# Gate matmuls of an RG-LRU stage: both neighbours' edges in one copied operand, and one buffer for modulation rows

## The chip, the cores and the metric

The kernel runs on one core of one Trainium2 chip. The metric is the device time of one execution of the whole program in microseconds (us), given as the median of several runs. The engines are PE (TensorE, the matmuls), DVE (VectorE), ACT (ScalarE), POOL (GpSimd) and SP (SyncE, which here only issues transfers). Each engine works through its own queue in order, and waits for the others by semaphores. Transfers are issued on the queues of SP, ACT and POOL.

## The reference

The program is a two-layer model for 512 tokens of width 1024: layer 0 mixes the tokens with an RG-LRU (a gated linear recurrence), layer 1 with attention, and each mixer is followed by a PEER feed-forward layer, which retrieves experts. Ahead of each of the four parts stands an adaptive norm whose shift, scale and gate are one matrix product of a single conditioning vector. The change lies in the RG-LRU:

```python
shift, scale, gate = ada_modulation(c, mw, mb)      # silu(c) @ mw + mb, split in three
h = rms_norm(x, g) * (1.0 + scale) + shift
xb, gb = jnp.split(h @ in_w, 2, axis=-1)            # 2 x 1408 columns
xb = causal_depthwise_conv(xb, conv_w, conv_b)
xblk = xb.reshape(B, S, 16, 88)                     # 16 blocks of 88 columns
r = sigmoid(einsum('bsnc,ncd->bsnd', xblk, ra_w).reshape(B, S, 1408) + ra_b)
i = sigmoid(einsum('bsnc,ncd->bsnd', xblk, ri_w).reshape(B, S, 1408) + ri_b)
log_a = -8.0 * softplus(-lam) * r
a = exp(log_a)
u = sqrt(-expm1(2.0 * log_a)) * (i * xb)
hs = associative_scan(a * h_prev + u)               # along the 512 tokens
y = (hs * gelu(gb)) @ out_w
x = x + gate * y
```

The matrices of the two gates `r` and `i` are block-diagonal: 16 blocks of 88 by 88. The kernel cuts the 1408 columns into 11 chunks of 128, so blocks cross the borders of chunks, and a chunk's gate needs some columns of the chunk before and of the chunk behind.

## The kernel before

**Layout and precision.** Activations lie transposed: 128 columns of the model on the partitions, 512 tokens along the free axis. Every fp32 operand is split in two parts, a high one (`hi`, made by ACT, L226) and the rest (`lo`, a subtraction on DVE, L227), and a product is three matmuls: hi·hi, lo·hi, hi·lo.

**Weights.** `Stream` holds the list of all weight tiles in the order of their use. SP loads them (`wraw`), a few ahead of use; ACT and DVE split each into `whi` and `wlo`. `lru_plan` writes that list for this stage: for each chunk two projection tiles of 128x1024, and for each chunk of the gates one tile of 128x768 (2 gates x 3 neighbours x 128 columns).

**The loop of the LRU stage** (`lru`, L607 to L630) goes over the 11 chunks j. `proj_t` (L423 to L425, tiles `pacc`) makes the convolution's input with 24 matmuls of 512 columns. ACT copies it to `xp`, DVE adds the four taps (L617, tile `xc`), and ACT and DVE split `xc` into `xh` and `xl`, four buffers each. A second `proj_t` makes the branch for the gelu (`ge`). After each even chunk j, `gates((j-2, j-1))` treats the two chunks before it. For a chunk o and each of the two gates, PE adds up the products of the chunks o-1, o and o+1 (L584 to L586, tiles `gps`), three each; the first and the last chunk have two operands only. ACT then takes tanh of both (`sg`, L588), a second tanh (`T`), exp, and sqrt (`m`, L596); DVE multiplies (L599 to L601), runs the recurrence as a scan (L603), multiplies by `ge`, and splits the result into `yhi` and `ylo`, the operands of the output projection.

**Background.** `Background.pump(LP)` takes steps of the generator `mod_gen` between the chunks. One step is one row of 128x1024 of a modulation matrix, of which 22 pass in this stage: 8 of the mixer's gate (`l_mix`), then 14 of the following norm (`l_ffn`). POOL's queue loads a row (tile `mw`, L185), DVE multiplies it with the conditioning vector and sums it (L192, called a dot below), two or three tiny DVE steps add the bias (L196 to L199), and then the load for a later row is issued. `MB = 2` is the number of buffers, so that one row is loaded while another is multiplied. Between the two groups `row_of` writes the mixer's gate to memory and reads it back as a broadcast row (`grow`, L211), also on POOL's queue. The dots are kept in program order; the rest of each engine's order is laid out by a scheduler when the program is built.

**Behind the stage** comes `out_proj`: POOL loads the four tiles of `x` (L115) into memory that the stage frees, then further rows of `mw`, and PE runs the output projection (L465, tiles `oacc`). Its weights are split on DVE, in DVE's queue among the dots and the additions to `x`.

Of the kernel before, what the change touches and what calls it, by code (L numbers as in the profile page):

```python
# [4 lines left out]
F32 = mybir.dt.float32  # L5
# [14 lines left out]
DR = 1408  # L20
NR = DR // 128
EPS = 1e-6
FH = 16
# [18 lines left out]
M2 = 18  # L42
MB = 2
LP = 1.2
# [473 lines left out]

def lru_plan(in_w, gates, out_w):

    plan = []
    for j in range(NR + 1):
        if j < NR:
            plan += [(in_w[j], (KD, 128), 2)]
        if j == NR or j and j % 2 == 0:
            plan += [(gates[o], (2, 3, 128), 1) for o in range(j - 2 + j % 2, j)]
    return plan + out_plan(out_w, NR)


def lru(g, h, head, conv, bias, lam, during, grow_fn, after):  # L530
# [3 lines left out]
    with pool(tc, name="lruy", bufs=1) as ly:  # L534
        yhi = ly.tile([128, NR, S], F32R, name="yhi")
        ylo = ly.tile([128, NR, S], F32R, name="ylo")
        with pool(tc, name="lru", bufs=1) as lp, pool(tc, name="lruw", bufs=2) as lw:
# [29 lines left out]
            with pool(tc, name="lps2", bufs=2, space=PSUM) as psum2:  # L567
                g.stream.third = (lw, 1)
                bg = Background(*during(lw))
                ge = {}  # L570
                xc, xh, xl = {}, {}, {}

                def gates(chunks):
# [3 lines left out]
                    for o in chunks:  # L577
                        gh, gl = g.stream.take()
                        ins = [i for i in (o - 1, o, o + 1) if 0 <= i < NR]
                        for w in range(2):  # L580
                            ps = psum2.tile([128, S], F32, name=f"gps{w}", tag=f"gps{w}")
                            for i in ins:
                                b = i - o + 1
                                nc.tensor.matmul(ps, gh[:, w, b, :], xh[i], start=(i == ins[0]), stop=False)  # L584
                                nc.tensor.matmul(ps, gh[:, w, b, :], xl[i], start=False, stop=False)
                                nc.tensor.matmul(ps, gl[:, w, b, :], xh[i], start=False, stop=(i == ins[-1]))  # L586
                            sg[o, w] = lw.tile([128, S], F32, name=f"sg{w}", tag=f"sg{w}")
                            A.activation(sg[o, w], ps, AF.Tanh, scale=0.5, bias=gb[:, w, o:o + 1])  # L588
# [18 lines left out]
                for j in range(NR):  # L607
# [8 lines left out]
                    for k in (2, 1, 0):  # L616
                        V.scalar_tensor_tensor(xc[j], xp[:, k:k + S], cv[:, j, k:k + 1], xc[j],  # L617
                                               op0=OP.mult, op1=OP.add)
                    xh[j] = lw.tile([128, S], F32R, name="xh", tag="xh", bufs=4)
                    xl[j] = lw.tile([128, S], F32R, name="xl", tag="xl", bufs=4)  # L620
                    split(g, xh[j], xl[j], xc[j])
                    bg.pump(LP)
# [707 lines left out]
def model(tc, *aps):  # L1330
# [4 lines left out]
    with ExitStack() as ctx:  # L1335
# [27 lines left out]
        def arg(p, *names):  # L1363
            return [a[p + n] for n in names]

        g.stream = Stream(g, lru_plan(*arg("lru_", "in", "gates", "out"))
                          + peer_plan(*arg("l0_", "qw", "sk", "uT", "v"))
# [18 lines left out]
def layouts(inp):  # L1386
# [30 lines left out]
    o["lru_bias"] = C(np.stack([f["l0_lru_ra_b"], f["l0_lru_ri_b"]]).reshape(2, NR, 128).transpose(2, 0, 1))  # L1417
    gates = np.zeros((NR, 128, 2, 3, 128), np.float32)
    for w, name in enumerate(("l0_lru_ra_w", "l0_lru_ri_w")):
        blk = f[name]  # L1420
        n, b = blk.shape[0], blk.shape[1]
        full = np.zeros((DR, DR), np.float32)
        for i in range(n):
            full[i * b:(i + 1) * b, i * b:(i + 1) * b] = blk[i]
        for oc in range(NR):
            for s in range(3):
                ic = oc + s - 1
                if 0 <= ic < NR:
                    gates[oc, :, w, s, :] = full[ic * 128:(ic + 1) * 128, oc * 128:(oc + 1) * 128]
    o["lru_gates"] = gates  # L1430
    o["lru_lam"] = cols(f["l0_lru_lambda"])
# [14 lines left out]
    for l in ("l0", "l1"):  # L1446
# [11 lines left out]
         *(p + s for p in ("l0_mix", "l0_ffn", "l1_mix", "l1_ffn") for s in ("_mw", "_mb", "_g")),  # L1458
         *("lru_" + n for n in ("in", "conv", "bias", "gates", "lam", "out")),
         *("fox_" + n for n in ("qk", "v", "f", "og", "fb", "qg", "kg", "out")),  # L1460
# [18 lines left out]
```

## Time and profile before

| | |
|---|---|
| median of 3 runs | 3129.46 us (3129.38 to 3132.22) |
| the profiled execution | 3133.16 us, span 3131.4, mean clock of PE 0.992 |
| PE busy | 3044.2 us, 97% of the span |
| DVE busy | 2560.7 us, 82% |
| ACT busy | 1469.5 us, 47% |
| POOL busy | 965.7 us, 31% |
| the LRU stage in the trace | from 56.4 to 219.9 us |

The span runs from the first to the last instruction of the profiled execution; its own time lies 1.8 us above that, and 3.7 us above the median. In a row of a timeline the first number is the start in us from the span's start, the second the time in us, then engine, line, operation, the tiles (out<-in) and their shapes; what stands in brackets is the idle time ahead of it and who ended it. In a row of waits the three numbers are the sum, the count and the longest wait. In a row of windows stand the stretch, its length, and the busy time of PE, PEld (the weight loads of PE), DVE, ACT and POOL with the number of instructions, then PE's granted clock, the DMA engines' mean busy share and the GB/s.

### The profile page before, as it was taken

The page shows a single profiled execution, that of the slowest core. Times are in us where ns is not written, and L with a number is a line of the kernel's source. Part 1 is how long each engine was busy: PE and PEld are TensorE (multiplying, and loading weights), DVE is VectorE, ACT ScalarE, POOL GpSimd, SP SyncE. Part 2 cuts the span into 40 slices and gives each one's busy share as a digit, 9 for nine tenths or more (in the row PEclk, how much of TensorE's full clock was granted, in tenths as well). Part 3 has the DMA queues.
Part 4 walks back from the last instruction along what each step waited for, and adds up shares of the span by engine and source line. Part 5 has one row for each costly group of instructions (what it writes and reads, how often), then busy time and mean ns, then how long its engine had stood idle before and what let it go on. Part 6 is the DMA issues. An engine that isn't in the chain of part 4 may idle for free.

```text
span 3131.4 us, 44513 instructions
## 1 busy us (share of the span) xinstructions
PE 3044.2 (97%) x16192; PEld 2675.4 (85%) x16192; DVE 2560.7 (82%) x5274; ACT 1469.5 (47%) x2129; POOL 965.7 (31%) x853
## 2 busy tenths in 40 slices
PE   7998999999999999999999999999999999999999
PEld 5876899988888888888777778999988888888888
DVE  7866889978988888887579976899879888888884
ACT  5763237873333333333458744267843333333332
POOL 0001430007654245452011102510037454544440
PEclk9999999999999999999999999999999999999999
DMA  7545245779999999997332243346699999999983
GB/s 270 170 170 169 98 149 180 270 292 388 403 373 362 366 367 354 368 347 269 115 119 96 82 148 120 123 150 241 245 370 398 354 372 345 349 335 345 362 310 118
DMA packets 300429, 818.99 MB, mean 262 GB/s; under 512 B 28848, under 2 KB 151728, under 8 KB 271664
## 3 DMA queue, kind: packets, MB, share of 16 engines
q1 hardware_dynamic: 168464, 388.79, 34.9%
q0 software_dynamic: 90272, 324.58, 27.5%
q10 hardware_dynamic: 41472, 102.78, 8.7%
q8 instruction: 127, 2.08, 0.3%
q14 instruction: 94, 0.77, 0.1%
HBM read 735.03 MB, written 81.02 MB: 261 GB/s over the span
## 4 chain that ended last, share of the span: by engine, by line
PE 70%; DVE 11%; DMA 4%; issue 2%; ACT 2%; POOL 1%; DVEq 0%; SPq 0%; ACTq 0%; POOLq 0%
PE vacc L1042 29%; PE pacc L423 11%; PE pacc L425 11%; PE pacc L424 11%; DVE wlo L227 3%; PE gps L906 2%; DMA wraw<-in_l_v_dram 2%; DVE rows L954 2%; DMA rows<-in_l_u_dram,ei 1%; DVE ge L817 1%; DVE pg L930 1%; PE tp L1299 1%; DVE p L919 1%; PE vacc L1139 0%; PE vacc L1141 0%
## 5 line engine op out<-in xcount | busy, mean ns | idle before, releaser
L226 ACT ACTIVATE whi<-wraw 128x1024 fp32r<-128x1024 f32 (+1 forms) x646 | 664.2, 1034 | 645.1 <-PE pacc L424 386.6
L423 PE MATMUL pacc<-hhi,whi 128*128 128x384 f32 (+1 forms) x2616 | 921.0, 352 | 11.8 <-ACT at L1022 7.1
L425 PE MATMUL pacc<-hhi,wlo 128*128 128x384 f32 (+1 forms) x2616 | 915.4, 350 | 5.0 <-DVE wlo L227 5.0
L424 PE MATMUL pacc<-hlo,whi 128*128 128x384 f32 (+1 forms) x2616 | 912.6, 349 | 0.0
L227 DVE TENSOR_TENSOR wlo<-wraw,whi 128x1024 fp32r<-128x1024 f32 (+1 forms) x580 | 700.3, 1211 | 216.7 <-ACT whi L226 216.3
L1042 PE MATMUL vacc<-whi,wl 128*128 128x512 f32 x1536 | 601.3, 391 | 3.0 <-DVE wl L1035 3.0
L1042 PE MATMUL vacc<-wlo,wh 128*128 128x512 f32 x1536 | 600.6, 391 | 1.5 <-DVE wlo L227 1.5
L1042 PE MATMUL vacc<-whi,wh 128*128 128x512 f32 x1536 | 598.1, 389 | 0.5 <-ACT whi L226 0.5
L423 PEld LDWEIGHTS pacc<-hhi,whi 128*128 128x128 f32 x2616 | 492.8, 188 | 41.8 <-ACT at L1022 8.1
L425 PEld LDWEIGHTS pacc<-hhi,wlo 128*128 128x128 f32 x2616 | 492.0, 188 | 32.7 <-DVE wlo L227 8.2
L424 PEld LDWEIGHTS pacc<-hlo,whi 128*128 128x128 f32 x2616 | 492.7, 188 | 28.8 <-issue 1.7
L1032 ACT ACTIVATE wh<-at 128x384 fp32r<-128x384 f32 x256 | 134.1, 525 | 747.0 <-DVE at L1028 448.7
L945 POOL DMA_INDIRECT rows<-in_l_v_dram,ei x256 | 357.1, 1395 | 380.4 <-DVE accg L966 340.5
L945 POOL DMA_INDIRECT rows<-in_l_u_dram,ei x256 | 372.1, 1454 | 262.0 <-DVE rows L954 209.8
L1042 PEld LDWEIGHTS vacc<-whi,wl 128*128 128x128 f32 x1536 | 288.6, 188 | 64.3 <-DVE wl L1035 4.1
L1042 PEld LDWEIGHTS vacc<-wlo,wh 128*128 128x128 f32 x1536 | 288.5, 188 | 59.8 <-DVE wlo L227 2.1
L1042 PEld LDWEIGHTS vacc<-whi,wh 128*128 128x128 f32 x1536 | 288.9, 188 | 58.2 <-ACT whi L226 1.3
L966 DVE SCALAR_TENSOR_TENSOR accg<-rows,act,accg 128x1024 f32<-128x1024 f32 x254 | 324.8, 1279 | 0.5
L954 DVE SCALAR_TENSOR_TENSOR rows<-rows,hn 128x1024 f32<-128x1024 f32 x256 | 305.1, 1220 | 11.3 <-DMA rows<-in_l_u_dram,ei 11.2
L1028 DVE TENSOR_TENSOR at<-at,gtile 128x384 f32<-128x384 f32 x256 | 141.0, 553 | 112.5 <-DMA at<-ascr 104.0
L908 ACT ACTIVATE st<-gps 128x512 f32<-128x512 f32 x192 | 186.6, 1111 | 33.7 <-PE gps L906 33.4
L227 POOL TENSOR_TENSOR wlo<-wraw,whi 128x1024 fp32r<-128x1024 f32 (+1 forms) x66 | 134.4, 2049 | 189.4 <-ACT whi L226 189.4
(296 smaller groups left out, 3380.1 us busy)
## 6 DMA issues: line engine op xcount, KB each, us to landing
wraw<-in_l_uT_dram SPq DMA_DIRECT2D x128, 1024.0 KB, 7.0
wraw<-in_l_v_dram SPq DMA_DIRECT2D x128, 1024.0 KB, 9.5
gscr<-st ACTq DMA_DIRECT2D x48, 1024.0 KB, 4.7
gtile<-gscr SPq DMA_DIRECT2D x90, 512.0 KB, 12.4
mw<-in_l_ffn_mw_dram POOLq DMA_DIRECT2D x48, 512.0 KB, 3.6
ascr<-at ACTq DMA_DIRECT2D x112, 192.0 KB, 3.1
at<-ascr ACTq DMA_DIRECT2D x112, 192.0 KB, 7.3
mw<-in_l_mix_mw_dram POOLq DMA_DIRECT2D x32, 512.0 KB, 6.5
```

The source lines that it names most:

```text
L226: g.nc.scalar.activation(hi, raw, AF.Copy)
L227: (eng or g.nc.vector).tensor_sub(lo, raw, hi)
L423: nc.tensor.matmul(ps, whi[:, k, :], hhi[:, k, :n], start=(k == 0), stop=False)
L424: nc.tensor.matmul(ps, whi[:, k, :], hlo[:, k, :n], start=False, stop=False)
L425: nc.tensor.matmul(ps, wlo[:, k, :], hhi[:, k, :n], start=False, stop=(k == KD - 1))
L908: A.activation(st[:, :, q * 4:q * 4 + 4].rearrange("p e t -> p t e"), gps, AF.Copy, scale=1.0 / GSCALE)
L945: i = nc.gpsimd.indirect_dma_start(out=rows, out_offset=None, in_=src, in_offset=bass.IndirectOffsetOnAxis(ap=ei[:, j:j + 1], axis=0))
L954: V.scalar_tensor_tensor(r, r, 1.0, hn, op0=OP.mult, op1=OP.mult, accum_out=act[:, j:j + 1]))
L966: tc.keep_in_program_order(V.scalar_tensor_tensor(acc, r, w, acc, op0=OP.mult, op1=OP.add))
L1028: pin(V.tensor_tensor(at.rearrange("p (b t) -> p b t", t=16), at.rearrange("p (b t) -> p b t", t=16), gts[c // 8][:, :, c % 8, :], op=OP.m ...
L1032: pin(A.activation(wh, at, AF.Copy))
L1042: T.matmul(acc[t][d], x[:, ts], y[:, d, :], start=(i == 0 and x is wh and y is vh), stop=(i == PK - 1 and x is wl))
```

## The change

It has two parts.

*Gates.* For the chunks 1, 3, 5, 7 and 9, the columns needed of the chunk before (40, 32, 24, 16, 8) and of the chunk behind (8, 16, 24, 32, 40) are 48 together. They get one operand of their own, `edge` (128 x 2 x 512, one buffer, set to zero once by DVE), instead of two full ones. `copy_edges` fills its first 48 partitions with two transfers from SBUF to SBUF on POOL's queue, hi and lo in one, 4 KB in each partition: the left one (L598 of the changed kernel) from chunk o-1, the right one (L599) from chunk o+1 as soon as that is split. `xh` and `xl` become one tile `xs`, so that a transfer takes both. These five chunks have two operands per gate in place of three: 30 matmuls fewer. The middle even chunks 2, 4, 6, 8 keep three. The gate weights lie in two arrays, with 512 columns where there are two operands (chunks 0, 10 and the five odd ones, seven tiles) and 768 in the other four.

*Modulation rows.* `MB` goes from 2 to 1: a row's buffer is loaded again only when the dot on it has ended.

```diff
-MB = 2
+MB = 1
...
+def edges(o):
+
+    if 0 < o < NR - 1:
+        left = o * 128 % GB
+        right = -(o + 1) * 128 % GB
+        if left + right <= 128:
+            return left, right
+    return None
...
-            plan += [(gates[o], (2, 3, 128), 1) for o in range(j - 2 + j % 2, j)]
+            plan += [(gates[o], (2, gates[o].shape[2], 128), 1) for o in range(j - 2 + j % 2, j)]
...
-                xc, xh, xl = {}, {}, {}
+                xc, xs = {}, {}
+                edge = lw.tile([128, 2, S], F32R, name="edge", tag="edge", bufs=1)
+                V.memset(edge.bitcast(F32), 0.0)
+
+                def parts(o):
+
+                    if edges(o):
+                        return xs[o], edge
+                    return [xs[i] for i in (o - 1, o, o + 1) if 0 <= i < NR]
+
+                def copy_edges(o):
+
+                    left, right = edges(o)
+                    nc.gpsimd.dma_start(edge[0:left], xs[o - 1][128 - left:128])
+                    nc.gpsimd.dma_start(edge[left:left + right], xs[o + 1][0:right])
...
-                        ins = [i for i in (o - 1, o, o + 1) if 0 <= i < NR]
+                        ins = parts(o)
...
-                            for i in ins:
-                                b = i - o + 1
-                                nc.tensor.matmul(ps, gh[:, w, b, :], xh[i], start=(i == ins[0]), stop=False)
-                                nc.tensor.matmul(ps, gh[:, w, b, :], xl[i], start=False, stop=False)
-                                nc.tensor.matmul(ps, gl[:, w, b, :], xh[i], start=False, stop=(i == ins[-1]))
+                            for b, x in enumerate(ins):
+                                nc.tensor.matmul(ps, gh[:, w, b, :], x[:, 0, :], start=(b == 0), stop=False)
+                                nc.tensor.matmul(ps, gh[:, w, b, :], x[:, 1, :], start=False, stop=False)
+                                nc.tensor.matmul(ps, gl[:, w, b, :], x[:, 0, :], start=False, stop=(b == len(ins) - 1))
...
-                    xh[j] = lw.tile([128, S], F32R, name="xh", tag="xh", bufs=4)
-                    xl[j] = lw.tile([128, S], F32R, name="xl", tag="xl", bufs=4)
-                    split(g, xh[j], xl[j], xc[j])
+                    xs[j] = lw.tile([128, 2, S], F32R, name="xs", tag="xs", bufs=4)
+                    split(g, xs[j][:, 0, :], xs[j][:, 1, :], xc[j])
+                    if j and edges(j - 1):
+                        copy_edges(j - 1)
```

New lines shift the numbers: L185 becomes L186, L192 becomes L193, L199 becomes L200, L211 becomes L212, L227 becomes L228, L423 to L425 become L424 to L426, L584 to L586 become L611 to L613, L617 becomes L644. Behind the stage the order of every engine is as before but for names. Within it three places matter.

The first place is DVE's queue around the split of chunk 6, before; `mw` is a modulation row, `mdot` its sum, `xl` the low part of the convolution's output, `wlo` that of a weight tile:

```order
L227 TENSOR_TENSOR xl<-xc,xh 128x512
L192 SCALAR_TENSOR_TENSOR mw,mdot<-mw,sc 128x1024 x2
L199 TENSOR_TENSOR col_l_ffn_117<-mdot,bias_l_ffn 128x1
L617 SCALAR_TENSOR_TENSOR xc<-xp,cv,xc 128x512
L196 TENSOR_SCALAR mdot<-mdot,bias_l_ffn 128x1
L617 SCALAR_TENSOR_TENSOR xc<-xp,cv,xc 128x512
L197 TENSOR_TENSOR col_l_ffn_125<-mdot,gain_l_ffn 128x1
```

The same rows of the modulation (117 and 125) in DVE's queue of the changed kernel:

```order
L193 SCALAR_TENSOR_TENSOR mw,mdot<-mw,sc 128x1024
L644 SCALAR_TENSOR_TENSOR xc<-xp,cv,xc 128x512
L200 TENSOR_TENSOR col_l_ffn_117<-mdot,bias_l_ffn 128x1
L228 TENSOR_TENSOR wlo<-wraw,whi 128x1024
L644 SCALAR_TENSOR_TENSOR xc<-xp,cv,xc 128x512
L639 MEMSET xp 128x3 x2
L193 SCALAR_TENSOR_TENSOR mw,mdot<-mw,sc 128x1024
L228 TENSOR_TENSOR xs<-xc,xs 128x512
```

Two dots that followed each other directly now have two steps of the convolution, a weight split and small steps between them, and the split of `xs`, which the right copy waits for, stands behind the second dot.

The second place is POOL's queue from the first modulation row of the stage to the loads of `x` behind it, before; `grow` is the broadcast gate row:

```order
L185 DMA mw<-in_l_mix_mw_dram 128x1024 x8
L185 DMA mw<-in_l_ffn_mw_dram 128x1024 x2
L211 DMA grow<-line 128x1024
L185 DMA mw<-in_l_ffn_mw_dram 128x1024 x12
L115 DMA x_1873<-in_x_dram 128x1024
```

The first rows of the same stretch of POOL's queue in the changed kernel, to the first copy behind `grow`:

```order
L186 DMA mw<-in_l_mix_mw_dram 128x1024
L598 DMA edge<-xs 40x1024
L186 DMA mw<-in_l_mix_mw_dram 128x1024 x3
L599 DMA edge<-xs 8x1024
L186 DMA mw<-in_l_mix_mw_dram 128x1024
L598 DMA edge<-xs 32x1024
L186 DMA mw<-in_l_mix_mw_dram 128x1024 x3
L599 DMA edge<-xs 16x1024
L186 DMA mw<-in_l_ffn_mw_dram 128x1024
L598 DMA edge<-xs 24x1024
L212 DMA grow<-line 128x1024
L186 DMA mw<-in_l_ffn_mw_dram 128x1024 x4
```

Ten copies now stand among the 22 row loads, each right copy (L599) directly behind a row load; one `l_ffn` row stands ahead of `grow` in place of two.

The third place is PE's queue at the last products of chunk 1, before; `gps_756` and `gps_768` are its two gates, `pacc` the projection of a later chunk:

```order
L423 MATMUL pacc<-hhi,whi 128x512
L584 MATMUL gps_756<-xh,whi 128x512
L584 MATMUL gps_768<-xh,whi 128x512
L424 MATMUL pacc<-hlo,whi 128x512
L425 MATMUL pacc<-hhi,wlo 128x512
L423 MATMUL pacc<-hhi,whi 128x512
L585 MATMUL gps_756<-xl,whi 128x512
L586 MATMUL gps_756<-xh,wlo 128x512
L585 MATMUL gps_768<-xl,whi 128x512
L586 MATMUL gps_768<-xh,wlo 128x512
```

The same place in PE's queue of the changed kernel, where the two gates are `gps_755` and `gps_764`:

```order
L424 MATMUL pacc<-hhi,whi 128x512
L425 MATMUL pacc<-hlo,whi 128x512
L611 MATMUL gps_755<-edge,whi 128x512
L612 MATMUL gps_755<-edge,whi 128x512
L613 MATMUL gps_755<-edge,wlo 128x512
L611 MATMUL gps_764<-edge,whi 128x512
L612 MATMUL gps_764<-edge,whi 128x512
L613 MATMUL gps_764<-edge,wlo 128x512
L426 MATMUL pacc<-hhi,wlo 128x512
```

The products that waited for chunk 2 stood 7 projection matmuls behind the others of chunk 1; those with `edge` stand 35 behind them, as one block of six.

More of the change, by code (lines that the diff above doesn't have):

```diff
@@ L21 @@
 NR = DR // 128
+GB = DR // 16
 EPS = 1e-6
@@ L516, in finish, with lru_plan @@
         self.credit = 0.0
-def lru_plan(in_w, gates, out_w):
+def edges(o):
[5 more added lines that the diff above has]
+    return None
+def lru_plan(in_w, three, two, out_w):
+    take = [iter(range(n)) for n in (three.shape[0], two.shape[0])]
+    gates = [three[next(take[0])] if 0 < o < NR - 1 and not edges(o) else two[next(take[1])] for o in range(NR)]
     plan = []
@@ L1364, in arg @@
             return [a[p + n] for n in names]
-        g.stream = Stream(g, lru_plan(*arg("lru_", "in", "gates", "out"))
+        g.stream = Stream(g, lru_plan(*arg("lru_", "in", "gates3", "gates2", "out"))
                           + peer_plan(*arg("l0_", "qw", "sk", "uT", "v"))
@@ L1417, in layouts @@
     o["lru_bias"] = C(np.stack([f["l0_lru_ra_b"], f["l0_lru_ri_b"]]).reshape(2, NR, 128).transpose(2, 0, 1))
-    gates = np.zeros((NR, 128, 2, 3, 128), np.float32)
+    gates = [np.zeros((128, 2, 3 if 0 < oc < NR - 1 and not edges(oc) else 2, 128), np.float32) for oc in range(NR)]
     for w, name in enumerate(("l0_lru_ra_w", "l0_lru_ri_w")):
@@ L1425, in layouts @@
         for oc in range(NR):
[L1426 to L1430, printed above, removed]
+            own, end = oc * 128, oc * 128 + 128
+            if edges(oc):
+                left, right = edges(oc)
+                gates[oc][:, w, 0, :] = full[own:end, own:end]
+                gates[oc][:left + right, w, 1, :] = np.concatenate(
+                    [full[own - left:own, own:end], full[end:end + right, own:end]])
+            else:
+                for s, ic in enumerate(i for i in (oc - 1, oc, oc + 1) if 0 <= i < NR):
+                    gates[oc][:, w, s, :] = full[ic * 128:(ic + 1) * 128, own:end]
+    for n in (2, 3):
+        o[f"lru_gates{n}"] = C(np.stack([x for x in gates if x.shape[2] == n]))
     o["lru_lam"] = cols(f["l0_lru_lambda"])
@@ L1458 @@
          *(p + s for p in ("l0_mix", "l0_ffn", "l1_mix", "l1_ffn") for s in ("_mw", "_mb", "_g")),
-         *("lru_" + n for n in ("in", "conv", "bias", "gates", "lam", "out")),
+         *("lru_" + n for n in ("in", "conv", "bias", "gates2", "gates3", "lam", "out")),
          *("fox_" + n for n in ("qk", "v", "f", "og", "fb", "qg", "kg", "out")),
```

## The prediction

> **What bounds the kernel now.** I read the page first, then the stage that the change touches: the windows from its start (56.4 us) to its last VectorE instruction (219.9 us), the waits of PE and DVE in it, and the timelines.
>
> The chain that ended last, by engine (page):
>
> ```profile
> PE 70%; DVE 11%; DMA 4%; issue 2%; ACT 2%; POOL 1%; DVEq 0%; SPq 0%; ACTq 0%; POOLq 0%
> ```
>
> The stage by its pairs of chunks, then the output projection (windows: length, busy time of PE, PEld, DVE, ACT, POOL, granted clock, DMA share):
>
> ```profile
> 56.40:96.90 40.50, 39.68 (x173) 32.02 (x172) 34.72 (x81) 27.29 (x41) 3.23 (x6) 1.00 0.46 164
> 96.90:127.50 30.60, 29.98 (x130) 23.75 (x129) 27.44 (x45) 23.04 (x31) 2.68 (x5) 1.00 0.70 208
> 127.50:158.40 30.90, 30.90 (x137) 25.38 (x136) 28.09 (x51) 21.75 (x29) 3.22 (x6) 1.00 0.52 182
> 158.40:188.90 30.50, 30.50 (x136) 25.13 (x135) 25.85 (x44) 21.73 (x29) 2.15 (x4) 1.00 0.40 131
> 188.90:219.90 31.00, 30.03 (x129) 23.67 (x128) 23.59 (x34) 23.43 (x30) 0.54 (x1) 1.00 0.31 102
> ```
>
> PE is full in this stage, at full clock, and DVE is second: 34.72+27.44+28.09+25.85+23.59 = 139.7 us busy of 163.5, so 23.8 us idle. PE's waits in the stage, all of them, and the largest of DVE's:
>
> ```profile
> PE oacc L465 <- DVE wlo L227: 0.9, 1, 0.9
> PE pacc L425 <- DVE wlo L227: 0.8, 1, 0.8
> PE gps L585 <- DVE xl L227: 0.5, 1, 0.5
> DVE m L599 <- ACT m L596: 11.2, 5, 4.5
> DVE sg L600 <- ACT sg L588: 5.8, 5, 2.0
> DVE wlo L227 <- ACT whi L226: 4.0, 5, 2.3
> DVE mw L192 <- DMA mw<-in_l_mix_mw_dram: 1.2, 1, 1.2
> ```
>
> So PE sets the pace by a small margin; most of DVE's idle time is waiting for a chain PE → ACT → m, and modulation rows cost it next to nothing. The end of the stage is DVE's: its last `ylo` frees the memory into which POOL loads `x`; these loads, the next modulation rows and DVE's in-order queue lead to the wait of 8.8 us in the output projection.
>
> ```profile
> 220.24 1.60 POOL L115 DMA_DIRECT2D x<-in_x_dram  x3 [1.67 <-DVE ylo L227]
> 248.38 0.80 PE L465 MATMUL oacc<-wlo,yhi 128*128 128x512 f32 x1 [8.80 <-DVE wlo L227]
> ```
>
> Hence only what makes DVE finish this stage earlier reaches the end. Behind it the instruction order is unchanged, so the rest of the program should move along.
>
> **The change, part by part.**
>
> *Matmuls removed.* Five chunks lose one of three operands: 5 x 2 gates x 3 products = 30. The 36 gate products of two chunks run from the first of these rows to the second:
>
> ```profile
> 158.47 0.40 PE L584 MATMUL gps<-xh,whi 128*128 128x512 f32 x1
> 166.72 0.40 PE L423 MATMUL pacc<-hhi,whi 128*128 128x512 f32 x1
> ```
>
> 8.25/36 = 0.229 us each; 30 x 0.229 = 6.9 us of PE, 1.4 per pair of chunks. An operand with 48 filled rows still streams 512 columns, so the remaining products cost as before. If nothing replaces PE as the bound, this is the gain; 156.6 us is then the stage.
>
> *Smaller weights.* Seven weight tiles shrink from 768 to 512 columns. DVE's steps, from start to start (timeline):
>
> ```profile
> 121.08 0.74 DVE L617 SCALAR_TENSOR_TENSOR xc<-xp,cv,xc 128x512 f32<-128x512 f32 x1
> 121.75 0.95 DVE L227 TENSOR_TENSOR wlo<-wraw,whi 128x768 fp32r<-128x768 f32 x1
> 122.62 0.69 DVE L227 TENSOR_TENSOR ylo<-T,yhi 128x512 fp32r<-128x512 f32 x1
> 123.22 1.22 DVE L192 SCALAR_TENSOR_TENSOR mw<-mw,sc 128x1024 f32<-128x1024 f32 x1
> 124.36 0.08 DVE L192 DVE_READ_ACCUMULATOR mw<-mw,sc 128x1 f32 x1
> ...
> 126.08 1.22 DVE L227 TENSOR_TENSOR wlo<-wraw,whi 128x1024 fp32r<-128x1024 f32 x1
> 127.22 0.69 DVE L227 TENSOR_TENSOR xl<-xc,xh 128x512 fp32r<-128x512 f32 x1
> 127.82 1.22 DVE L192 SCALAR_TENSOR_TENSOR mw<-mw,sc 128x1024 f32<-128x1024 f32 x1
> ```
>
> Split of 768: 0.87; of 512: 0.60; so DVE gains 7 x 0.27 = 1.9 us. ACT's half and the smaller loads are beside other work: nothing. The memset of `edge` (as long as another 1024-column step, 1.14) stands where DVE waits 2.83 us for `gbias`: nothing; without that cover 1.1.
>
> ```profile
> 55.30 0.18 DVE L564 TENSOR_SCALAR gbias<-gbias 128x22 f32<-128x22 f32 x1 [2.83 <-DMA gbias<-in_lru_bias_dram]
> ```
>
> *One buffer for modulation rows.* With two, the next row lies ready; with one, a dot (L192) frees the buffer, POOL issues the load, and the next dot waits for it in DVE's queue, with weight splits, `xs` and the recurrence behind it.
>
> In DVE's queue around chunk 6, the first place shown with the change, the pair of dots was pulled apart, but only two steps of the convolution and a weight split stand between them: 0.67+1.14+0.67 and some small ones, 2.6 us. What is needed between two dots is read from these rows (POOL's and DVE's timelines, and the landing times of the stage's 20 row loads):
>
> ```profile
> 124.74 0.54 POOL L185 DMA_DIRECT2D mw<-in_l_ffn_mw_dram  x1 [8.12 <-DVE mw L192]
> 129.31 1.23 DVE L192 SCALAR_TENSOR_TENSOR mw<-mw,sc 128x1024 f32<-128x1024 f32 x1 [0.26 <-DMA mw<-in_l_ffn_mw_dram]
> DMA to landing us min/median/max: 3.5/4.5/6.8
> ```
>
> The dot ended at 124.4, POOL issued 0.3 later, and the row was there 4.6 after that. I take 4.2 for the landing: loads now come singly, which speaks for the low end 3.5, but weight loads still cross many, which speaks for the median. So 0.3+4.2+0.05 = 4.55 us are needed. Counting DVE's new order by the durations above (and 1.22 for a scan or a step of 1024), 15 of the 21 successive pairs of dots have less between them: 4.2, 2.0, 3.2, 3.7, 3.15, 1.8, 3.85, 2.6, 2.5, 3.3, 2.4, 1.4, 4.0, 2.5, 3.7, in sum 44.3 us. They wait 15 x 4.55 - 44.3 = 24.0 us. With 3.5 it is 14.0 (four gaps or so wait no more), with 5.1 it is 38.
>
> *The `grow` load*, in POOL's queue: it waits for a slow small DMA, and now the second ffn row stands behind it. First the end of the last mix dot, from DVE's timeline, then POOL's:
>
> ```profile
> 102.50 0.08 DVE L192 DVE_READ_ACCUMULATOR mw<-mw,sc 128x1 f32 x1
> ...
> 115.55 0.54 POOL L211 DMA_DIRECT2D grow<-line  x1 [12.14 <-DMA line<-gate_l_mix]
> 116.08 0.54 POOL L185 DMA_DIRECT2D mw<-in_l_ffn_mw_dram  x1
> ```
>
> From the dot's end (102.5) to the issue of that row are 13.6 us; it lands after 4.2 to 6.8: about 18 to 20 us. By the same count DVE has 16 us of other steps: 2 to 4 us of waiting, taken as 3.
>
> *The copies.* Ten copies enter POOL's queue, and PE waits for them at its last products of each odd chunk. In POOL's queue, the second place shown with the change, the right copy (L599) stands directly behind a row load; in PE's, the third place, the products with `edge` stand in one block of six, in chunk 1 35 matmuls (8 us) behind the chunk's others.
>
> The left copy (L598) waits for PE to be done with the chunk before, a pair of chunks earlier: free, and the row load behind it waits for a later dot anyway. The right copy is urgent. Nearest rows for its landing: small copies of the same queue at 1.8 and 3.3, and a row alone at 3.5, in traffic at 6.8.
>
> ```profile
> cx<-cl POOLq DMA_DIRECT2D x1, 32.0 KB, 1.8
> qx<-cx POOLq DMA_DIRECT2D x16, 8.0 KB, 3.3
> ```
>
> I take 3.5, nearest to the load that it follows. Then the products (1.4) and ACT's chain to `m` follow, 4.8 us by these rows:
>
> ```profile
> 166.28 0.67 ACT L588 ACTIVATE sg<-gps,gbias 128x512 f32<-128x512 f32 x1
> 171.04 1.30 DVE L599 SCALAR_TENSOR_TENSOR m<-sg,m 128x512 f32<-128x512 f32 x2 [1.94 <-ACT m L596]
> ```
>
> Meanwhile DVE is held by its next two dots: in chunk 7 the copy path takes 7.1 us and the landing, DVE needs 12.0, so a landing to 4.9 is free; for chunks 1, 3, 5, 9 the same count gives 5.8, 3.5, 3.9, 4.6. At 3.5 the copies cost nothing on DVE; PE stands there for some us, which only gives back what it had saved.
>
> **The sum.** DVE: 139.7 - 1.9 + 24.0 + 3 = 164.8 us, its former waits for `m` and `sg` being swallowed by the new ones; PE: 156.6. The later one counts: 164.8 - 163.5 = +1.3 us. The profiled execution (3133.2, span 3131.4) becomes 3134.5; the median lies 3.7 lower, so 3129.5 + 1.3 = 3130.8, say 3131.
>
> **The rivals.**
>
> *PE stays the bound: 3122.6.* At a landing of 3.5, DVE needs 137.8+14.0+3 = 154.8 us, less than PE's 156.6: all 6.9 us are gained. For it: single loads without weight traffic did land in 3.5. Against: the median. The Trainium skill, page "DMA: Bandwidth & Descriptors", section "Anatomy of one DMA — SWDGE (gpsimd) path", fits such a load as 2.0 us and its bytes at 436 GB/s: an estimate of 3.2 us for a row, below every load of this stage.
>
> *The right copy lands late, slower: 3142.* If it takes 6.8, because it shares a queue with the row before it, the five chunks exceed what is free by 1.0+3.3+2.9+1.9+2.2 = 11.3 us: +12.6 in all. It decides from about 5 us on (+4). For it: it always follows a row load. Against: the small copies above.
>
> *Rows land at 5.1 or more: 3145.* The 15 gaps then cost 38 us: +15. For it: the maximum of 6.8; against: two of those loads were paired, which no longer happens. The skill's first page, "Trainium Kernel Development and Optimization", section "Best Practices", says to double-buffer so that transfers overlap compute; the 1.2 us that DVE waited for mix rows with two buffers agree, and one buffer for rows is the opposite.
>
> That the change doesn't take place is excluded: PE's queue has 30 rows fewer.
>
> **How the numbers follow.** No change: 0.2% is 6.3 us, about what a measurement of this kernel tells from none. My forecast 0.5 (with landings of 3.9 to 4.5 it runs from -3 to +6); full gain 0.2, just over the bound; late copy 0.2; late rows 0.1. Faster 0.2, same 0.5, slower 0.3. The range goes from the full gain, 3122.4, up to 3139, which holds the lesser half of the two slow cases.
>
> **What would show it.** DVE's waits for `mw` by DMA rise from 1.5 us to some 20 or more in the stage; its waits for `m` and `sg` fall well below 17; the last `ylo` stands near 221. PE has new waits at the `edge` products or on `xs`, some 7 us in sum. If the `mw` waits stay under 14 us and PE stands nowhere, the full gain is right; if DVE waits for `m` as before and PE stands over 2 us at each `edge`, it is the late copy. It is wrong altogether if the later stages change their length.

## The result, and the profile after

The changed kernel takes 3153.55 us (median of 6 runs, 3146.81 to 3161.15), the kernel before, run beside it again, 3131.36 (6 runs): a ratio of 1.0059 with a 95% interval of 1.0040 to 1.0077, or 18.5 us slower by the ratio; the two medians lie 22.2 us apart. The forecast was 3131, at most 3139. The profiled execution of the changed kernel is the longest of its six, 3161.15 us with a span of 3159.4, so its whole span is compared with care; the LRU stage is what counts.

In this document the stage is measured from the first step of the convolution to the end of the last `ylo`: 56.48 to 219.94 us before, 163.5 us. After, from DVE's timeline:

```profile
56.84 0.75 DVE L644 SCALAR_TENSOR_TENSOR xc<-xp,cv,xc 128x512 f32<-128x512 f32 x1 [0.89 <-ACT xc L642]
...
238.07 0.69 DVE L228 TENSOR_TENSOR ylo<-T,yhi 128x512 fp32r<-128x512 f32 x1
```

The stage takes 181.9 us, 18.4 more, as much as the ratio gives for the whole program. What stands behind the stage is longer in this execution too, 2920.6 us against 2911.5; in the runs below that part lies between 2910.2 and 2921.5 us, with either number of buffers, so nothing is read from it. Behind the stage the output projection waits as before, 9.5 us at its second half in place of 8.8, from PE's timeline:

```profile
267.89 0.80 PE L466 MATMUL oacc<-wlo,yhi 128*128 128x512 f32 x1 [9.49 <-DVE wlo L228]
```

The stage in the windows of the changed kernel (length, busy time of PE, PEld, DVE, ACT, POOL, granted clock, DMA share, GB/s), first as a whole, then the two stretches where something happens:

```profile
56.84:238.75 181.91, 162.71 (x668) 129.47 (x667) 138.96 (x251) 116.15 (x158) 17.76 (x33) 0.94 0.47 146
111.00:126.00 15.00, 15.00 (x64) 12.25 (x63) 3.11 (x6) 6.93 (x10) 1.08 (x2) 0.94 0.68 113
126.00:155.00 29.00, 20.73 (x73) 15.37 (x72) 23.69 (x41) 15.71 (x21) 2.92 (x6) 0.82 0.43 152
```

From 111 to 126 us DVE works 3.1 us of 15, and in the 29 us behind that PE works 20.7, at a clock of 0.82. Nothing of the kind stood in the kernel before. The waits of the stage, DVE's and then PE's (sum, count, longest):

```profile
DVE mw L193 <- DMA mw<-in_l_ffn_mw_dram: 25.8, 10, 11.9
DVE mw L193 <- DMA mw<-in_l_mix_mw_dram: 6.6, 5, 2.7
DVE wlo L228 <- ACT whi L227: 4.4, 3, 2.9
DVE m L626 <- ACT m L623: 3.2, 3, 1.5
DVE xs L228 <- ACT xs L227: 1.2, 2, 0.6
DVE wlo L228 <- PE gps L613: 1.2, 1, 1.2
DVE xc L644 <- ACT xc L642: 0.9, 1, 0.9
```

```profile
PE gps L611 <- DMA edge<-xs: 7.9, 5, 2.5
PE gps L613 <- DVE wlo L228: 5.9, 1, 5.9
PE gps L611 <- ACT sg L615: 2.8, 1, 2.8
PE oacc L466 <- DVE wlo L228: 1.6, 1, 1.6
PE gps L611 <- ACT xs L227: 1.0, 1, 1.0
```

Both engines' accounts close on the stage within half a microsecond. DVE: 139.0 us busy, 32.4 of waits for rows, 10.9 of other waits, 182.3. PE: 162.7 busy and 19.2 of waits, 181.9. PE saved 30 matmuls and is nevertheless busy 1.6 us longer than before, since it ran part of the stage at a lower clock.

The longest wait, 11.9 us, belongs to one row. POOL's, SP's and DVE's timelines around it:

```profile
109.89 0.56 POOL L186 DMA_DIRECT2D mw<-in_l_ffn_mw_dram  x1 [3.27 <-DVE gate_l_mix L200]
111.16 0.53 POOL L598 DMA_DIRECT2D edge<-xs  x1 [0.70 <-PE gps L613]
123.03 0.55 POOL L212 DMA_DIRECT2D grow<-line  x1 [11.35 <-DMA line<-gate_l_mix]
```

```profile
109.82 0.38 SPq L210 DMA_DIRECT2D line<-gate_l_mix  x1
```

```profile
124.64 1.23 DVE L193 SCALAR_TENSOR_TENSOR mw<-mw,sc 128x1024 f32<-128x1024 f32 x1 [11.85 <-DMA mw<-in_l_ffn_mw_dram]
```

The first `l_ffn` row was issued at 109.89 and was there at 124.64, 14.75 us later; no row took more than 6.8 before. SP issued `line` at the same moment: 4 KB, written to memory as 1024 pieces of 4 bytes, which were there only when POOL could issue `grow`, at 123.03. That the two met is in the order of the queues: `line` writes out `gate_l_mix`, and POOL's bracket shows that the same step of DVE (L200) released the row's load. The transfers of these 13 us, from the DMA view of that window:

```profile
DMA packets 1203, 0.67 MB, mean 51 GB/s; under 512 B 1054, under 2 KB 1054, under 8 KB 1189
```

51 GB/s in place of the stage's 146, though a row of 512 KB, a copy of 96 KB and a weight tile of 1024 KB had been issued by 112.3. In the kernel before, `line` was nearly as slow (POOL waited 12.1 us for it), but the two rows beside it had been issued 1.7 and 0.5 us ahead of it, into two buffers, and DVE waited for neither.

### The profile page after: what moved, and what is told of

Its sections match the earlier page's. It is cut to its first block, busy times and chain, and to the rows that moved or that the text cites. A ratio compares the mean times of both kernels' runs of the same rounds, so it can differ in the third digit from the quotient of the medians.

```text
span 3159.4 us, 44485 instructions
## 1 busy us (share of the span) xinstructions
PE 3046.3 (96%) x16162; PEld 2676.1 (85%) x16162; DVE 2560.4 (81%) x5275; ACT 1468.1 (46%) x2129; POOL 966.9 (31%) x863
## 4 chain that ended last, share of the span: by engine, by line
PE 71%; DVE 14%; DMA 6%; issue 6%; ACT 3%; POOL 1%; SPq 0%; DVEq 0%; POOLq 0%; ACTq 0%
PE vacc L1070 29%; PE pacc L424 11%; PE pacc L426 11%; PE pacc L425 11%; DVE wlo L228 3%; PE gps L934 2%; DVE rows L982 2%; DMA wraw<-in_l_v_dram 2%; DVE ge L845 1%; DMA wraw<-in_l_uT_dram 1%; DVE pg L958 1%; DMA mrow<-in_l_mix_mw_dram 1%; PE oacc L466 1%; PE oacc L467 1%; PE oacc L465 1%
## 5 line engine op out<-in xcount | busy, mean ns | idle before, releaser
L227 ACT ACTIVATE whi<-wraw 128x1024 fp32r<-128x1024 f32 (+1 forms) x646 | 662.3, 1031 | 641.6 <-PE pacc L425 369.9
L424 PE MATMUL pacc<-hhi,whi 128*128 128x384 f32 (+1 forms) x2616 | 921.9, 352 | 14.2 <-ACT at L1050 7.6
L426 PE MATMUL pacc<-hhi,wlo 128*128 128x384 f32 (+1 forms) x2616 | 916.2, 350 | 9.4 <-DVE wlo L228 9.4
L425 PE MATMUL pacc<-hlo,whi 128*128 128x384 f32 (+1 forms) x2616 | 913.1, 349 | 0.0
L228 DVE TENSOR_TENSOR wlo<-wraw,whi 128x1024 fp32r<-128x1024 f32 (+1 forms) x580 | 698.0, 1207 | 223.1 <-ACT whi L227 217.9
L424 PEld LDWEIGHTS pacc<-hhi,whi 128*128 128x128 f32 x2616 | 493.3, 189 | 45.2 <-ACT at L1050 8.6
L426 PEld LDWEIGHTS pacc<-hhi,wlo 128*128 128x128 f32 x2616 | 492.5, 188 | 37.3 <-DVE wlo L228 12.8
L425 PEld LDWEIGHTS pacc<-hlo,whi 128*128 128x128 f32 x2616 | 493.3, 189 | 28.8 <-issue 1.7
L228 POOL TENSOR_TENSOR wlo<-wraw,whi 128x1024 fp32r<-128x1024 f32 (+1 forms) x66 | 134.4, 2048 | 190.2 <-ACT whi L227 190.2
```

Source lines behind the costliest of these rows:

```text
L227: g.nc.scalar.activation(hi, raw, AF.Copy)
L228: (eng or g.nc.vector).tensor_sub(lo, raw, hi)
L424: nc.tensor.matmul(ps, whi[:, k, :], hhi[:, k, :n], start=(k == 0), stop=False)
L425: nc.tensor.matmul(ps, whi[:, k, :], hlo[:, k, :n], start=False, stop=False)
L426: nc.tensor.matmul(ps, wlo[:, k, :], hhi[:, k, :n], start=False, stop=(k == KD - 1))
```

## The experiments

Two theories to begin with. **A:** the loss is the single buffer's, above all the one row that meets the 4-byte write. **B:** the loss is the copies', for which PE waits, and behind PE the gates' chain. All runs in one table. Stage and waits come from one profiled execution each, the ratio from all executions. The stage is in us, then DVE's waits for rows and PE's waits for the copies in the stage, then the ratio to the kernel before with its interval. Where a kernel leaves part of the computation out, its section says so.

| kernel | stage | rows | copies | ratio |
|---|---|---|---|---|
| before | 163.5 | 1.5 | | |
| after | 181.9 | 32.4 | 7.9 | 1.0059 (1.0040 to 1.0077) |
| 1 before, one buffer | 171.6 | 24.6 | | 1.0036 (1.0017 to 1.0055) |
| 2 after, two buffers | 181.6 | 5.3 | 14.4 | 1.0055 (1.0038 to 1.0073) |
| 3 after, `line` in 32-byte pieces | 171.5 | 22.9 | 7.9 | 1.0022 (1.0006 to 1.0039) |
| 4 after, no copies | 169.8 | 29.1 | | 1.0021 (1.0004 to 1.0037) |
| 5 after, two buffers, `line` turned | 168.8 | 4.9 | 4.3 | 1.0027 (1.0015 to 1.0040) |
| 6 as 5, copies on SP's queue | 172.6 | 4.9 | 7.1 | 1.0020 (1.0008 to 1.0032) |
| 7 as 5, no copies | 159.9 | 4.4 | | 0.9999 (0.9984 to 1.0014) |
| 8 before, `line` turned | 164.1 | 2.2 | | 0.9994 (0.9979 to 1.0009) |
| 9 as 5, copies by ACT | 164.9 | 4.4 | 3.7 | 1.0012 (0.9999 to 1.0025) |
| 10 before, one buffer, `line` turned | 165.2 | 18.1 | | 1.0004 (0.9989 to 1.0019) |
| 11 after, copies by ACT | 171.0 | 23.7 | 5.5 | 1.0032 (1.0018 to 1.0046) |

### 1. The single buffer alone

```diff
 (before)
-MB = 2
+MB = 1
```

> The kernel before with one buffer for modulation rows and nothing else: no edge operand, no copies. Theory A (the loss comes from the single buffer: a dot waits for its row, and one row meets the slow 4-byte write of `line`): DVE waits about 30 us for `mw` in the LRU stage, its last `ylo` stands 12 to 19 us later than before, the time is 3142 to 3150 us. Theory B (the loss comes from the copies on POOL's queue, for which PE waits and behind PE ACT and DVE): no copies, so the stage stays at 163 to 167 us and the time within 4 us of before.

The stage took 171.6 us, 8.1 more than before. DVE's waits for rows and the former waits of the gates' chain:

```profile
DVE mw L192 <- DMA mw<-in_l_ffn_mw_dram: 17.9, 7, 5.4
DVE mw L192 <- DMA mw<-in_l_mix_mw_dram: 6.7, 4, 3.5
DVE sg L600 <- ACT sg L588: 4.2, 3, 2.0
DVE m L599 <- ACT m L596: 1.4, 2, 0.7
```

So the single buffer costs time by itself, against B, but in the stage not half of the loss, less than A expected (its range for the time, 3142 to 3150, held: 3145): of 24.6 us of waits 15.6 replace waits that were there before (22.9 us of other waits before, 7.3 now). The longest wait, 5.4 us, was not for the row beside `line`, as A had it. That row was issued 0.4 us ahead of `line` and landed in 3.6 us; DVE waited for the next one, which stood behind `grow` in POOL's queue.

### 2. Two buffers again

```diff
 (after)
-MB = 1
+MB = 2
-                edge = lw.tile([128, 2, S], F32R, name="edge", tag="edge", bufs=1)
+                edge = ylo[:, NR - 2:NR, :]
```

> The changed kernel with two buffers for modulation rows again; the memory comes from `edge` lying in the last two chunks of `ylo`, which are not written before the end of the stage. Copies and 30 fewer matmuls stay. Theory A: the waits for `mw` fall under 5 us, but the right copy of chunk 3 now stands behind `grow` in POOL's queue and waits with it for `line`, so PE stands there for some 5 to 10 us; stage 163 to 172 us, time 3128 to 3138. Theory B: all ten copies are still there, so the stage is as long as in the changed kernel, 178 us or more, time 3147 or more.

The waits for rows fell to 5.3 us and the stage stayed at 181.6: A's range for the stage failed, and B's came out. But it is not the ten copies of themselves. With two buffers the scheduler set the right copy of chunk 3 behind `grow` in POOL's queue; POOL's timeline, then PE's:

```profile
116.32 0.54 POOL L212 DMA_DIRECT2D grow<-line  x1 [13.06 <-DMA line<-gate_l_mix]
116.87 0.51 POOL L599 DMA_DIRECT2D ylo<-xs  x1
```

```profile
123.41 0.77 PE L611 MATMUL gps<-ylo,whi 128*128 128x512 f32 x1 [9.35 <-DMA ylo<-xs]
```

The same `line` now holds up a copy in place of a row, as A's text had expected of chunk 3. Run 5, which differs from this one in `line` alone, has a stage 12.8 us shorter.

### 3. The gate column written in larger pieces

```diff
 (after; at the mixer's gate alone, the switch for it is left out here)
-    nc.sync.dma_start(line.rearrange("k p -> p k"), col)
+    nc.sync.dma_start(line.rearrange("k p -> (k p)").rearrange("(p k) -> p k", k=KD), col)
```

> The changed kernel, but the mixer's gate goes to memory as 128 pieces of 32 bytes, not as 1024 of 4 bytes; the row read back then has its columns in another order, so the gate's columns are permuted in this part of the computation. Order of the engines unchanged. Theory A: the row issued beside `line` lands in 4 to 6 us in place of 14.75, DVE's longest wait of 11.9 us falls to 3 or less, the stage is 9 to 12 us shorter (170 to 173 us), time 3139 to 3145. Theory B, and every theory in which `line` plays no part: that wait and the stage stay within 2 us of the changed kernel.

Of the transfers issued between 109.7 and 112.5 us, the row and `line`, with KB and time to landing:

```profile
mw<-in_l_ffn_mw_dram POOLq DMA_DIRECT2D x1, 512.0 KB, 4.6
line<-gate_l_mix SPq DMA_DIRECT2D x1, 4.0 KB, 1.4
```

`line` lands in 1.4 us in place of 13.2, the row beside it in 4.6 in place of 14.75, and the wait for it is 2.0:

```profile
114.38 1.23 DVE L193 SCALAR_TENSOR_TENSOR mw<-mw,sc 128x1024 f32<-128x1024 f32 x1 [1.96 <-DMA mw<-in_l_ffn_mw_dram]
```

The order of the engines is that of the changed kernel, the same bytes are moved, and the stage is 10.4 us shorter. That the 4-byte write is what slowed the row is shown by this run.

### 4. No copies

```diff
 (after)
-                        copy_edges(j - 1)
+                        pass
```

> The changed kernel without the ten copies: `edge` stays zero, so what the neighbouring chunks add to the gates of the odd chunks is left out. The 30 matmuls fewer and the single buffer stay. Theory A: DVE's waits for `mw` stay at 25 us or more, the stage is at most 5 us shorter than in the changed kernel, time 3146 or more. Theory B: PE's 7.9 us of waits for `edge` go, the stage falls by 8 us or more, time under 3143.

169.8 us, 12.1 less than the changed kernel: B's number for the stage. A failed here, in its claim that the copies cost 5 us at most. But the run takes out more than the copies' price. Without them the step that released the first `ffn` row was the dot itself, so the row went 0.9 us ahead of `line` (108.92) and landed in 4.0 us. The longest wait, 7.2 us in place of 11.9, was for the row behind `grow`. POOL's and DVE's timelines:

```profile
107.98 0.54 POOL L186 DMA_DIRECT2D mw<-in_l_ffn_mw_dram  x1 [4.98 <-DVE mw L193]
121.64 0.54 POOL L212 DMA_DIRECT2D grow<-line  x1 [13.13 <-DMA line<-gate_l_mix]
122.17 0.54 POOL L186 DMA_DIRECT2D mw<-in_l_ffn_mw_dram  x1
```

```profile
128.29 1.23 DVE L193 SCALAR_TENSOR_TENSOR mw<-mw,sc 128x1024 f32<-128x1024 f32 x1 [7.24 <-DMA mw<-in_l_ffn_mw_dram]
```

A kernel without copies waits for nothing of the chunk behind, so it is a lower bound, not a version to be had.

### 5. Both other costs taken out

From here on theory A is that three prices add up; C, that the copies cost nothing once nothing else is late. The gate column is turned on DVE and leaves in 32 pieces of 128 bytes, for the grow rows of all four parts:

```diff
 (run 2)
-    nc.sync.dma_start(line.rearrange("k p -> p k"), col)
+    wide = g.small.tile([128, 32], F32, name="wide", tag="wide", bufs=1)
+    nc.vector.memset(wide, 0.0)
+    nc.vector.tensor_copy(wide[:, 0:KD], col)
+    turned = g.small.tile([128, 32], F32, name="turned", tag="turned", bufs=1)
+    nc.vector.transpose(turned, wide)
+    for b in range(4):
+        nc.sync.dma_start(line[:, b * 32:b * 32 + 32], turned[b * 32:b * 32 + KD, :])
```

> The edges of the changed kernel with both other costs taken out: two buffers for modulation rows (`edge` in the last chunks of `ylo`), and the gate column turned on DVE in blocks of 32x32 and written as 32 pieces of 128 bytes, at all four places. Theory A (the price of the single buffer, of the slow `line` and of the copies add up): what is left is PE's wait for the right copies, five of 1 to 3 us and the slower clock behind some of them, against 6.9 us of matmuls saved: stage 160 to 167 us, time within 5 us of before. Theory C (the copies cost nothing once nothing else is late): PE's waits for `edge` under 2 us, stage 156 to 159, time 5 to 8 us below before.

The stage took 168.8 us, a little over A's range, the time 8.5 us over before by the ratio, outside A's 5, and C is out. Against run 7, which has no copies, the stage is 8.9 us longer, and PE's waits for the copies are only 4.3 us. The rest is read as the later place of the products in PE's queue, with ACT and DVE behind them: DVE's waits for ACT's `m` and `whi` are 11.8 and 6.8 us here, 8.3 and 3.7 in run 7. No run shows this place by itself. The last product of chunk 1, here and in run 7, from PE's timelines:

```profile
80.87 0.39 PE L619 MATMUL gps<-ylo,wlo 128*128 128x512 f32 x1
```

```profile
72.77 0.39 PE L619 MATMUL gps<-ylo,wlo 128*128 128x512 f32 x1
```

The product stands 8.1 us later, but the first scan behind it only 1.8 us (88.8 against 87.0); by the second pair the scans are 7.8 us apart. And at the last pair, where no projection is left to stand between, a copy of 40 rows took 7.7 us from POOL's issue to PE's start:

```profile
194.87 0.53 POOL L605 DMA_DIRECT2D ylo<-xs  x1 [2.30 <-DVE xs L234]
```

```profile
202.53 0.50 PE L617 MATMUL gps<-ylo,whi 128*128 128x512 f32 x1 [2.69 <-DMA ylo<-xs]
```

The other four right copies of this run landed in 2.1 to 3.4 us. This one is the largest, 160 KB, and ran while the DMA engines were busy for 0.80 of the time, against 0.19 to 0.76 beside the others. Which of the two made it slow is open.

### 6. The copies on another queue

"The kernel before" in this expectation is the kernel of run 5.

```diff
 (run 5, both copies)
-nc.gpsimd.dma_start(edge[0:left], xs[o - 1][128 - left:128])
+nc.sync.dma_start(edge[0:left].bitcast(F32), xs[o - 1][128 - left:128].bitcast(F32))
```

> As the kernel before, but the ten copies are issued on SP's queue, between the weight loads, not on POOL's between the row loads. Theory A: the copies' price is their landing time, so if a copy lands sooner from this queue (under 3 us) PE's waits for them shrink and the stage is 2 to 4 us shorter; if it lands as late as on POOL's queue, stage and time are the same within 2 us, or longer by a wait behind a weight load. Theory C: no difference, as the copies cost nothing on either queue.

172.6 us: the stage is longer by 3.8. The time is not: 3141.1 against 3143.8 us, with intervals that overlap. SP stood 13.9 us in sum waiting for the splits that four right copies need, with weight loads behind, and DVE's waits for `whi` rose from 6.8 to 11.6 us. Whether a copy's data waited behind a weight tile is not shown. PE stood for two copies, which took 3.7 and 9.0 us from issue to PE's start, where the same two took 3.5 and 7.7 on POOL's queue. So no copy was seen to land sooner from this queue.

### 7. Without copies, the other costs taken out

The run that this expectation compares with is run 5. The edit is that of run 4, made on run 5.

> The kernel of the first run of this call without the ten copies: what the neighbours add to the gates of the odd chunks is left out. Two buffers, turned `line`, 30 matmuls fewer. Theory A: without the waits for copies the stage is 5 us or more shorter than with them, 155 to 159 us, time 4 to 8 us below before: the full worth of the 30 matmuls. Theory C: the same as with copies, within 1.5 us. If the stage stays at 161 us or more, the 30 matmuls are worth nothing here, since DVE or ACT is then the bound.

159.9 us, just past A's range. The stage in windows:

```profile
57.12:217.00 159.88, 155.52 (x669) 125.76 (x668) 138.13 (x254) 115.01 (x158) 11.87 (x22) 0.99 0.46 156
```

So the copies, with the wait for the chunk behind that comes with them, cost 8.9 us of stage. The shorter gates without them are worth 4.2 (164.1 in run 8), not 6.9: PE's busy time falls to 155.5 us, and DVE with its waits does not follow all the way. In the time of the whole program even that does not show, against A's 4 to 8 us: 0.9999, with an interval of 3 in a thousand.

### 8. The turned column in the kernel before

> The kernel before with the turned gate column alone, at all four places: three operands, two buffers, no copies. Theory A: the 4-byte write hurts only who waits for a transfer issued beside it; with two buffers no row is waited for there, so the stage stays at 162 to 165 us and the time within 3 us of before. Rival D: the 4-byte write costs time in the kernel before as well, through late weight tiles: stage 158 to 161, time 3 to 10 us lower.

The edit is that of run 5 on the kernel before. 164.1 us and a ratio of 0.9994: A is right, D is out. The 4-byte write costs nothing here, where nobody waits for a transfer issued beside it.

### 9. The edges copied by ACT

```diff
 (run 5; the edge weights are laid out to match, and `edge` is no longer set to zero)
-                    nc.gpsimd.dma_start(edge[0:left], xs[o - 1][128 - left:128])
-                    nc.gpsimd.dma_start(edge[left:left + right], xs[o + 1][0:right])
+                    A.activation(edge[64:128], xs[o - 1][64:128], AF.Copy)
+                    A.activation(edge[0:64], xs[o + 1][0:64], AF.Copy)
```

> Two buffers, the turned gate column, and the edges copied by ACT itself: `edge` keeps the rows on their own partitions (the upper 64 of the chunk before, the lower 64 of the chunk behind, zero weights for rows that are not needed), so two ACT copies of 64x1024 take the place of two transfers. Theory A (the price of the copies is the time until they land): ready about 1.5 us after the split in place of 2.4 to 7.6, stage 158 to 163 us, time within 4 us of before. Rival E (the price lies in the order, in the products with `edge` standing as a block behind others): the stage stays at 166 us or more, as with the transfers.

164.9 us, 3.9 less than with transfers, between the two expectations. The landing of the transfers is thus worth about 4 us of the 8.9, in the stage; in the ratios, 1.0012 against 1.0027, it does not stand clear of the intervals. What the other 5 are made of stays open: ACT has 125.5 us of work in place of 116.3, PE still waits 3.7 us for its copies, and any valid version has to wait for the chunk behind, which run 7 does not.

### 10. The single buffer without the 4-byte write

> The kernel before with one buffer for modulation rows and the turned gate column: the single buffer's price without the 4-byte write. Theory A: the longest wait for `mw` (5.4 us with the 4-byte write) falls to 2 us, the sum of the waits from 24.6 to some 18 to 21 us, the stage from 171.6 to 165 to 168 us. Rival D (the whole price of the single buffer is that one row): stage 164.5 or less. Rival: the 4-byte write plays no part without the copies: stage 171 or more.

Runs 1 and 5's edits to `MB` and `line`, on the kernel before. 165.2 us, 1.1 more than run 8, as A had it but for the longest wait, 3.6 us in place of 2. The waits for rows and those of the gates' chain are

```profile
DVE mw L192 <- DMA mw<-in_l_ffn_mw_dram: 12.5, 7, 3.4
DVE mw L192 <- DMA mw<-in_l_mix_mw_dram: 5.6, 3, 3.6
DVE sg L606 <- ACT sg L594: 3.6, 3, 1.4
DVE m L605 <- ACT m L602: 1.6, 2, 0.9
```

18.1 us of waits for rows almost wholly replace other waits. In this kernel the single buffer costs next to nothing until a row is late.

### 11. The changed kernel with ACT's copies

> The changed kernel itself (one buffer, 4-byte write) with ACT's copies in place of the ten transfers. Theory A: as the changed kernel without copies, where the stage was 169.8 us: 168 to 172 us, time 3138 to 3145. Rival E: nothing gained by it, stage 178 us or more.

171.0 us, as A had it, 10.9 less than the changed kernel; the time, 3148, is above A's 3145. As in run 4, taking the transfers out shortens the stage by more than with two buffers (3.9 in run 9), and here too the meeting with `line` went with them: the first `ffn` row goes 0.9 us ahead of it and lands in 4.1 us, and the longest wait is 4.5 us, for the row behind `grow`, in place of 11.9.

**What follows.** Along one chain of kernels the 18.4 us come apart in whole: the turned column by itself +0.6 (run 8), the 30 matmuls -4.2 (run 7), the copies +8.9 (run 5), the single buffer +2.7 (run 3, whose `line` goes in 32-byte pieces), the 4-byte write +10.4 (the changed kernel). In the ratios only two of these terms stand clear of the intervals, the copies (run 7 to run 5) and the 4-byte write (run 3 to the changed kernel). Since the parts act on each other, another chain gives other shares. The 4-byte write costs 12.8 us with copies and two buffers (run 5 to run 2), 6.4 with one buffer and no copies (run 10 to run 1), and nothing with two buffers and no copies (run 8). The single buffer costs 8.1 us where the 4-byte write is left in and no copies are there (run 1), but 0.3 where the copies are there too (run 2 to the changed kernel). No version here is faster than the kernel before.

## Why the prediction was wrong

*What bounds the stage* was right: DVE's last `ylo` set its end, and the stage is longer by as much as the program is by the ratio (18.4 and 18.5 us).

*The waits for rows between neighbouring dots* were right. Forecast 24.0 us in 15 waits; measured 32.4 in 15, of which 11.9 at the row beside `line`, so 20.5. The landing of 4.2 us taken for a row is about what the runs with one buffer show (run 3: 4.2 and 4.3, the medians of the two groups of rows).

*The `grow` load* is the first step that failed. It was put as "2 to 4 us of waiting, taken as 3", by a row behind `grow` in POOL's queue. In the changed kernel the row that suffered stood ahead of `grow`, and not because of the queue: it shared the moment of issue with `line`, and DVE waited 11.9 us for it. Run 3 shows the size: 10.4 us of stage. The place that the forecast named is not empty: in runs 1, 4 and 11, where the first `ffn` row goes ahead of `line`, DVE waits 5.4, 7.2 and 4.5 us for the row behind `grow`. The step had the right cause, a slow `line`, and missed that it slows the transfers beside it and not only POOL's queue behind it. The profile of before had shown signs of that. The slowest row of the stage there, 6.8 us, was the one issued 0.5 us ahead of `line`, where the prediction blamed a pair of loads, and the gates' weight tile issued 1.1 us behind `line` took 10.7 us.

*The copies* are the second: "At 3.5 the copies cost nothing on DVE". In the changed kernel three of the right copies reached PE after these times (POOL's and PE's rows):

```profile
177.57 0.51 POOL L599 DMA_DIRECT2D edge<-xs  x1
...
207.89 0.53 POOL L599 DMA_DIRECT2D edge<-xs  x1 [1.51 <-DVE xs L228]
```

```profile
108.57 0.50 PE L611 MATMUL gps<-edge,whi 128*128 128x512 f32 x1 [2.25 <-DMA edge<-xs]
181.94 0.50 PE L611 MATMUL gps<-edge,whi 128*128 128x512 f32 x1 [2.47 <-DMA edge<-xs]
214.84 0.77 PE L611 MATMUL gps<-edge,whi 128*128 128x512 f32 x1 [1.27 <-DMA edge<-xs]
```

4.4 us for the copy issued at 177.57, 6.9 for the last; that of 106.12 took 2.4, those of chunks 1 and 5 took 3.8 and 4.4. By the forecast's own count of what is free (5.8, 3.5, 3.9, 4.9 and 4.6 for chunks 1 to 9) only chunks 5 and 9 are over, by 0.5 and 2.3 us, so late landing explains a part. The rival "the right copy lands late" had that part, but at landings like these it would have expected little. Run 5 shows 8.9 us with only 4.3 of waits for copies. The products' later place in PE's queue had been noted, 35 matmuls or 8 us in chunk 1, and not priced; how much of the rest is due to it stays open.

*The sum's last clause*, that DVE's former waits are "swallowed by the new ones", nearly holds without copies (run 4: 3.6 us of other waits left; runs 1 and 10, where PE keeps its 30 matmuls, some 7) and fails with them: 10.9 us of other waits stood beside the 32.4, and 10.2 in run 3, without the slow `line`. In the forecast's terms: DVE 139.0 us busy instead of 137.8, rows 20.5 instead of 24.0, the row at `line` 11.9 instead of 3, other waits 10.9 instead of 0; 182.3 instead of 164.8. So two terms were mis-sized, 3 against 11.9 and 0 against 10.9, and their sum is more than either slow rival, 3142 and 3145, had allowed for.

*The matmuls saved* were counted right, 30, but no version here that computes the whole is faster by them; without copies they, with the smaller weight tiles, are worth 4.2 us (run 7), where 6.9 had been counted.

*The rival on late rows* had one as a general slowness of 5.1 us or more. Rows did not land late in general, as the medians above show.

## What to carry to other kernels

With one buffer, each load is on the path, so the slowest transfer that any load of the ring can meet sets the price, not the median: look for small-element transfers near them before a buffer is given up. When a copy is put between two steps, ask also for the place that the dependent instructions get in their queue, not only for the landing. And saved matmuls pay only as far as the next engine follows, which a kernel that leaves the new cost out shows in one run. Such a kernel can change the order elsewhere too, as runs 4 and 11 did, so see first whether the other waits stayed where they were.

## What was not expected of the hardware

A write of 4 KB in pieces of 4 bytes took 13.2 us, in pieces of 32 bytes 1.4 us. While the first kind ran, large transfers issued behind it were slow. In the changed kernel the row issued 0.07 us behind it, on another queue, took 14.75 us. In run 4 the row issued 0.9 us ahead of it landed in 4.0 us and a weight tile issued 1.7 us behind it in 14.4 (KB, time to landing):

```profile
mw<-in_l_ffn_mw_dram POOLq DMA_DIRECT2D x1, 512.0 KB, 4.0
line<-gate_l_mix SPq DMA_DIRECT2D x1, 4.0 KB, 12.2
wraw<-in_lru_in_dram SPq DMA_DIRECT2D x1, 1024.0 KB, 14.4
```

A row issued only 0.5 us ahead took 6.8 us in the kernel before and 10.1 in run 2.

PE's granted clock can fall to half after waits of 2 to 3 us. Stretches of 3.4 us around two waits for copies in the changed kernel, of 2.25 us (to 108.57) and of 2.47 us (to 181.94); PE's busy time is second, its clock third from the end:

```profile
105.80:109.20 3.40, 1.15 (x6) 0.64 (x5) 2.69 (x4) 1.77 (x2) 0.51 (x1) 1.00 0.41 147
109.20:112.60 3.40, 3.40 (x10) 2.68 (x9) 2.19 (x5) 2.39 (x4) 1.09 (x2) 0.52 0.20 7
112.60:116.00 3.40, 3.40 (x16) 2.74 (x16) 0.19 (x1) 3.38 (x6) 0.00 (x0) 0.98 0.21 29
```

```profile
177.60:181.00 3.40, 1.87 (x9) 1.21 (x7) 1.48 (x2) 1.46 (x2) 0.48 (x1) 1.00 0.69 190
181.00:184.40 3.40, 2.46 (x11) 2.04 (x12) 1.61 (x4) 1.46 (x2) 1.06 (x2) 1.00 0.03 7
```

The shorter wait was followed by 3.4 us at half clock, in which PE did 10 matmuls in place of 16. The longer one cost no clock. So the length of a wait alone does not decide it, and what does is not shown here. Over the stage PE was busy 162.7 us, where 30 matmuls less than before would be 161.1 - 6.9 = 154.2: 8.5 us went to the clock. The windows at half clock (from 109.3, 133.2 and 211.7 us) hold 16.9 us of busy PE, of which half, 8.4, agrees. The Trainium skill, page "TensorE: Matmul & The Clock Gate", section "Part 1: The HAM clock gate", tells of a half rate after an idle window of about 3.4 us. The half rate and the 3.4 us agree with these rows; that the window has to be idle throughout does not, since PE was busy for 1.15 us of it.
